# A macaron block with a recurrent mixer on one core: the mixer's TensorE order written out by hand, paired channel blocks, a split-row inverse, and chain steps moved to ScalarE

## The chip, the cores and the metric

The kernel runs on one core of one Trainium2 chip. The metric is device time in microseconds (us) of one execution. The engines are TensorE (PE: matmuls, and PEld: its weight loads), VectorE (DVE), ScalarE (ACT), GpSimd (POOL) and SyncE (SP), which issues the weight loads from DRAM.

## The reference

One transformer block on 256 tokens of width 2048, all in float32: a half-weighted SwiGLU, a mixer, and a second half-weighted SwiGLU, each between RMS norms.

```python
def _wkv7_scan(r, w, k, v, a, b):          # per head, state 64 x 64
    def step(state, inp):
        r_t, w_t, k_t, v_t, a_t, b_t = inp
        sa = jnp.einsum('bhvk,bhk->bhv', state, a_t)
        state = (state * w_t[:, :, None, :] + sa[..., None] * b_t[:, :, None, :]
                 + v_t[..., None] * k_t[:, :, None, :])
        return state, jnp.einsum('bhvk,bhk->bhv', state, r_t)
...
def _hybrid_mixer(u, w_in, ...):
    p = u @ w_in                            # 2048 -> 8480 columns
    z_a, z_b, g_a, g_b = jnp.split(p, IN_SPLITS, axis=-1)
    y_a = _rwkv7_branch(z_a, ...) @ w_proj_a
    y_b = _pool_branch(z_b, pool_w, pool_scale) @ w_proj_b
    m = jax.nn.sigmoid(g_a) * y_a + jax.nn.sigmoid(g_b) * y_b
    return m @ w_out
...
def reference(x, ...):
    f = _swiglu(_rmsnorm(h, ln_ffn1_pre[l]), ffn1_gate[l], ffn1_up[l], ffn1_down[l])
    h = h + 0.5 * _rmsnorm(f, ln_ffn1_post[l])
    mx = _hybrid_mixer(_rmsnorm(h, ln_mix_pre[l]), w_in[l], ...)
    h = h + _rmsnorm(mx, ln_mix_post[l])
    f = _swiglu(_rmsnorm(h, ln_ffn2_pre[l]), ffn2_gate[l], ffn2_up[l], ffn2_down[l])
    return h + 0.5 * _rmsnorm(f, ln_ffn2_post[l])
```

The recurrent branch has 16 heads of 64. It takes r, k, v, a decay, a gate and a learning rate from `z_a` after a token shift, runs the scan, normalizes, and adds a bonus. The pool branch subtracts each channel from its mean over the last 2, 4, 8 or 16 tokens (one window for each of four groups of 256 channels) and multiplies each group with a 256 x 256 matrix.

## The kernel before

**Products in three passes.** Every float32 weight tile (128 x 1024 numbers, 512 KB) is loaded by SyncE into one of four buffers (`w32`), cast on ScalarE to a high part `wH` (L101), and the rest `wL` is taken on VectorE (L102), into one of five buffers each. A product is then three matmuls, high by high, low by high, high by low (`mm3`, L109 to L111, 512 columns of output; L174 to L176 in the channel-major form, 256 columns). The casts and splits carry a high scheduling priority (`BOOST`).

**Stages.** Feed-forward 1 runs up to about 750 us of the span, the mixer from about 753 to 1420 us, feed-forward 2 after it. The change touches the mixer alone.

**The mixer.** `gemm_ch` makes channel-major blocks of 256 columns for the recurrent branch (the z blocks for k, v and r of each half of the heads) and for the pool windows; each block holds two PSUM banks, out of four for such products. `gemm_tok` makes the token-major gates and projections. `rwkv(hf, ...)` is the recurrent chain of one half, 8 heads. It replaces the 256-step scan by four chunks of 64 tokens:

- `pw`, `pa`: small products for decay and learning rate, sigmoids, a running sum, two exponentials;
- `pn`, GpSimd's power (L620), `pk`: the norm of k, turned back into channel-major form (L615 to L630);
- `pV`: transposes of v; `pA` (L706): products of the chunk's rows, masked into Xab, Xrb; `pB` (L720): transposes; `pb`: the bonus;
- the inverse of unit triangular matrices: four part transposes (L733), then 31 steps of a product (L740) and a sum (L742) on VectorE, two transposes back (L746, L747), and `pM`, `pX` to join 32 x 32 blocks into 64 x 64;
- the recurrence over four chunks: `pU` (L782), a copy (L789), `pSa` (L793), copies (L794, L795), `pS` (L800), the state update (L804, L805), `pY`, and the group norm;
- `pg`, `pT`: gate product and transposes back, and the branch's output `yT`.

The pool branch: `pool_window` computes a group's block, its product with the norm (L516), window sums (L522) and small fixes for the first tokens (L528 to L534), then the high and low parts `mxT` (L535, L536). `pool_mix` multiplies with the group's matrix (outputs `yb`, L547, L548). Group g's `pool_mix` is issued after group g+1's window; that of the last group is put off (`s.after`) until the next `gemm_ch` is done.

**What sets the order.** The source names the stages as `"a0 p a1 b0 b1 b2 b3"` (chain of half 0, pool, chain of half 1, then four blocks of the second projection), then four gate blocks. The order on every engine is made by the framework's scheduler, which plays the program through a model of the chip and takes instructions by readiness and priority. So TensorE's chain matmuls and the other products, called fillers here, are mixed by the scheduler. At run time each engine executes its instructions in that order.

Of the kernel before, what the change touches and what calls it, by code (L numbers as in the profile page):

```python
# [15 lines left out]
P = 128  # L16
# [18 lines left out]
ORDER = "a0 p a1 b0 b1 b2 b3"  # L35
# [9 lines left out]
class Block:  # L45
    def __init__(s, tc, ctx):
# [4 lines left out]
        s.after = []  # L51
# [98 lines left out]
    def gemm_pair(s, w, cols, at, KT, kh, evacs):  # L150

        pss = [[s.pm.tile([P, 512], F32, tag="mm", name=s.nm("mm")) for _ in range(2)]
               for _ in cols]
        for k0, k1 in ((0, kh), (kh, KT)):
            for i, c0 in enumerate(cols):
                for k, wH, wL in s.load_w(w, k0, k1 - k0, c0, 512):
                    xH, xL = at(k)
                    for h in range(2):
                        s.mm3(pss[i][h], xH[:, h * P:h * P + P], xL[:, h * P:h * P + P],
                              wH, wL, k == 0, k == KT - 1)  # L160
        for i in range(len(cols)):
            for h in range(2):
                evacs[i](h, pss[i][h])

    def gemm_ch(s, w, c0, cw, at, KT, evac, kstep):
        blocks = [(b, min(P, cw - b)) for b in range(0, cw, P)]
        pss = [s.pm.tile([P, 512], F32, tag="mm", name=s.nm("mc")) for _ in blocks]
        for k0 in range(0, KT, kstep):
            for k, wH, wL in s.load_w(w, k0, min(kstep, KT - k0), c0, cw):
                xH, xL = at(k)  # L170
                for (b, m), ps in zip(blocks, pss):
                    o = ps[:m, :S]
                    h_, l_ = wH[:, b:b + m], wL[:, b:b + m]
                    s.nc.tensor.matmul(o, h_, xH, start=k == 0, stop=False)  # L174
                    s.nc.tensor.matmul(o, l_, xH, start=False, stop=False)  # L175
                    s.nc.tensor.matmul(o, h_, xL, start=False, stop=k == KT - 1)  # L176
        with s.tc.high_priority(offset=BOOST):
            for i, (b, m) in enumerate(blocks):
                evac(i, pss[i][:m, :S])
        while s.after:  # L180
            s.after.pop()()
# [143 lines left out]
    def setup_mixer(s, prm):  # L325
# [40 lines left out]
        for h in range(2):  # L366
            for q, op in ((0, ALU.is_gt), (1, ALU.is_ge)):
                a = m[h * 64:h * 64 + 64, q]
                nc.gpsimd.affine_select(out=a, in_=a, compare_op=op, fill=0.0, base=0,
                                        pattern=[[1, C]], channel_multiplier=-1)  # L370
        s.bones = s.const([P, P], "bones")
# [3 lines left out]
        s.zi = 0  # L375
        s.zb = [s.const([P, S + 16], f"zb{i}") for i in range(2)]
        for z in s.zb:
            nc.gpsimd.memset(z[:, :16], 0.0)
# [4 lines left out]
    def shift(s, ps, m, mc, out):  # L383

        nc = s.nc
        z = s.tmp("z")[:m, :S]
        nc.vector.tensor_tensor(out=z, in0=ps, in1=s.rsb[:m], op=ALU.mult)
        zm = s.zb[s.zi % 2][:, 15:]
        s.zi += 1
        nc.scalar.activation(out=zm[:m, 1:], in_=z, func=AF.Copy,  # L390
                             scale=s.col["mu"][:m, mc:mc + 1])
        nc.vector.scalar_tensor_tensor(out=out, in0=z, scalar=s.col["omu"][:m, mc:mc + 1],
                                       in1=zm[:m, :S], op0=ALU.mult, op1=ALU.add)

    def mixer(s, prm, uT, rs, resid, emit, gpost, reload):
# [29 lines left out]
        def ev_l(i, ps):  # L425
            m = ps.shape[0]
            s.shift(ps, m, 24 + i, lz[:m, i])
            if i == 0:
                nc.scalar.activation(out=lz[:64, 0], in_=lz[:64, 0], func=AF.Tanh)
            else:  # L430
                nc.scalar.activation(out=lz[:m, i], in_=lz[:m, i], func=AF.Sigmoid)
        s.gemm_ch(w_in, 3 * W, 288, at, NKD, ev_l, 4)

        yT = [[s.unit((P, 4, S), F32R, n_) for n_ in ("yH", "yL")] for _ in range(2)]

        def branch_a(hf):
            z = {}
            for nme, zc in (("k", 1), ("v", 2), ("r", 0)):
                z[nme] = s.unit((P, 4, S), F32, "z" + nme)
                for b in range(2):  # L440
                    c0 = zc * W + hf * 512 + b * 256

                    def ev_z(i, ps):
                        s.shift(ps, P, c0 // P + i, z[nme][:, b * 2 + i])
                    s.gemm_ch(w_in, c0, 256, at, NKD, ev_z, 8)
            for t in yT[hf]:
                nc.scalar.copy(t[:, 0, :1], s.ident[:, :1])
            s.rwkv(hf, z["r"], z["k"], z["v"], lz, prm, *yT[hf])
# [7 lines left out]
        def branch_b(c):  # L456
            if c == 0:
                sg = [sgb0[:, 0], sgb0[:, 1]]
            else:
                sg = [s.tmp("sgb"), s.tmp("sgb")]  # L460
                s.gemm_tok(w_in, GB + c * 512, at, NKD, ev_sig(lambda h: sg[h]))
# [4 lines left out]
            while s.after:  # L466
                s.after.pop()()
            s.gemm_tok(prm["w_proj_b"], c * 512, at_b, NKW, ev_pb)

        for step in ORDER.split():  # L470
            if step == "p":
                mix = None
                for g, win in enumerate(POOL_WINDOWS):
                    nxt = s.pool_window(g, win, at, w_in)
                    if g:
                        pT.append(s.pool_mix(g - 1, mix, prm["pool_w"]))
                    mix = nxt
                s.after.append(lambda: pT.append(s.pool_mix(3, mix, prm["pool_w"])))
            elif step[0] == "a":
                branch_a(int(step[1]))  # L480
            else:
                branch_b(int(step[1]))

        sga = []
        for c in range(4):
            sg = s.unit((P, 2, 512), F32, "sga")
            sga.append(sg)
            s.gemm_tok(w_in, GA + c * 512, at, NKD, ev_sig(lambda h: sg[:, h]))
# [16 lines left out]
        s.gemm_pair(prm["w_proj_a"], (0, 512), at_a, NKW, 4, (ev_pa(0), ev_pa(1)))  # L505
# [4 lines left out]
    def pool_window(s, g, win, at, w_in):  # L510
        nc = s.nc
        mxT = s.unit((P, 2, 2, S), F32R, "mxT")

        def ev_b(i, ps):
            zp = s.zb[i]
            nc.vector.tensor_tensor(out=zp[:, 16:], in0=ps, in1=s.rsb, op=ALU.mult)  # L516
            cur = zp
            st = 1
            while st < win:
                nx = s.tmp("pl")[:, :S + 16]  # L520
                lo = 16 - (win - 2 * st)
                nc.vector.tensor_tensor(out=nx[:, lo:], in0=cur[:, lo:],  # L522
                                        in1=cur[:, lo - st:S + 16 - st], op=ALU.add)
                cur = nx
                st *= 2
            n = win - 1
            fx = s.small(16, "fx", bufs=2)[:, :n]
            nc.vector.tensor_tensor(out=fx, in0=cur[:, 16:16 + n], in1=s.rcp[:, :n],  # L528
                                    op=ALU.mult)
            nc.vector.tensor_tensor(out=fx, in0=fx, in1=zp[:, 16:16 + n], op=ALU.subtract)  # L530
            mx = cur[:, 16:]
            nc.vector.scalar_tensor_tensor(out=mx, in0=mx, scalar=1.0 / win,
                                           in1=zp[:, 16:], op0=ALU.mult, op1=ALU.subtract)
            nc.vector.tensor_copy(mx[:, :n], fx)  # L534
            nc.scalar.copy(mxT[:, 0, i], mx)  # L535
            nc.vector.tensor_tensor(out=mxT[:, 1, i], in0=mx, in1=mxT[:, 0, i].bitcast(F32),  # L536
                                    op=ALU.subtract)
        s.gemm_ch(w_in, RCOLS + g * 256, 256, at, NKD, ev_b, 8)
        return mxT

    def pool_mix(s, g, mxT, pool_w):
# [3 lines left out]
        def ev(i, ps):  # L545
            sc = s.col["pool_scale"][:, 2 * g + i:2 * g + i + 1]
            nc.scalar.activation(out=yb[:, 0, i], in_=ps, func=AF.Copy, scale=sc)  # L547
            nc.vector.scalar_tensor_tensor(out=yb[:, 1, i], in0=ps, scalar=sc,  # L548
                                           in1=yb[:, 0, i].bitcast(F32),
                                           op0=ALU.mult, op1=ALU.subtract)  # L550
        s.gemm_ch(pool_w[g], 0, 256, lambda k: (mxT[:, 0, k], mxT[:, 1, k]), 2, ev, 2)
        return yb[:, 0], yb[:, 1]

    def rwkv(s, hf, r, k, v, lz, prm, yH, yL):
# [25 lines left out]
        sw = reg(0, 4, S)  # L580
        for q in range(2):
# [22 lines left out]


        kk = reg(3, 4, S)
# [16 lines left out]
        nbf = nb.rearrange("p a b -> p (a b)")  # L623
        for q in range(2):
# [10 lines left out]
        for i in range(4):  # L635
            V.tensor_scalar(out=k2[:, i], in0=a[:, i], scalar1=col("k_a", i),
                            scalar2=col("oka", i), op0=ALU.mult, op1=ALU.add)
# [12 lines left out]
        E, O = slice(0, 64), slice(64, 128)  # L650
        t5 = (2, NCH, 2, C)
        BK = [reg(7, *t5), reg(8, *t5)]
        AR = [[reg(9, *t5), reg(10, *t5)], [reg(11, *t5), reg(12, *t5)]]
        EVs, ODs = reg(13, 4, NCH, C), reg(14, 4, NCH, C)
        Xab, Xrb = reg(4, 16, C), reg(5, 16, C)
        BKt = [reg(1, *t5), reg(2, *t5)]

        for q in range(2):
            pb = s.psum("pb").rearrange("p (i t) -> p i t", i=2)
            for i in range(2):  # L660
# [299 lines left out]
```

## Time and profile before

| | us |
|---|---|
| median of 3 runs | 2156.44 (2155.68 to 2157.66) |
| the profiled execution, its own time | 2156.19 |
| its span, first to last instruction | 2154.4 |

| engine | busy us | share of the span | instructions |
|---|---|---|---|
| TensorE matmul | 2114.6 | 98% | 11077 |
| weight loads | 1774.9 | 82% | 11077 |
| VectorE | 1288.9 | 60% | 1609 |
| ScalarE | 1086.2 | 50% | 1516 |
| GpSimd | 78.2 | 4% | 164 |

The mean granted TensorE clock of the execution is 0.992 of full speed. In the profile, L12 is line 12 of the kernel; a row of groups has line, engine, operation, output <- inputs, shape, count, then busy us and mean ns of one, then idle time of the engine before them and what ended it. Buffers are told by the program's names without their numbers: `R` is any of the chain's fifteen work tiles, `mc` a channel-major and `mm` a token-major PSUM tile.

### The profile page before, as it was taken

To read this page: it belongs to the slowest core of one execution; us is meant where nothing else is said; L and a number is where in the kernel's file an instruction comes from. 1 tells how busy PE (TensorE), PEld (TensorE's weight loads), DVE (VectorE), ACT (ScalarE), POOL (GpSimd) and SP (SyncE) were. 2 spreads that over 40 slices of the span, in tenths; PEclk is the share of its full clock that TensorE was granted. 3 is DMA by queue.
4 is the path that set the end of the run, shared out by engine and by line. 5 is a ranking of instruction groups with operands and counts; after the bars stand their busy time and mean duration, and the time that the engine had idled before them with its cause. 6 is when DMAs were issued, how large, how long until landed. Compare 5 with 4: busy or idle time off the path is not lost.

```text
span 2154.4 us, 28711 instructions
## 1 busy us (share of the span) xinstructions
PE 2114.6 (98%) x11077; PEld 1774.9 (82%) x11077; DVE 1288.9 (60%) x1609; ACT 1086.2 (50%) x1516; POOL 78.2 (4%) x164
## 2 busy tenths in 40 slices
PE   8999999999999999889999999999999999999998
PEld 6888888888888799889788778878888888888886
DVE  5556555555444556997689656565556555654444
ACT  6565556555444554444454434455565556554442
POOL 1000000000000100101110110010000000000000
PEclk9999999999999999999999999999999999999999
DMA  7656666667666666255556666656667666676664
GB/s 234 195 177 207 195 195 186 198 205 242 195 195 192 194 173 182 84 157 164 147 153 179 178 223 193 192 179 202 194 177 213 193 191 184 206 252 192 193 193 136
DMA packets 223219, 406.06 MB, mean 188 GB/s; under 512 B 12991, under 2 KB 48969, under 8 KB 223081
## 3 DMA queue, kind: packets, MB, share of 16 engines
q1 hardware_dynamic: 216937, 383.11, 58.9%
q0 software_dynamic: 6144, 21.11, 2.7%
q8 instruction: 87, 1.43, 0.3%
q14 instruction: 51, 0.42, 0.1%
HBM read 395.78 MB, written 8.39 MB: 188 GB/s over the span
## 4 chain that ended last, share of the span: by engine, by line
PE 90%; DVE 6%; issue 2%; ACT 1%; DMA 1%; POOL 0%; DVEq 0%; POOLq 0%; SPq 0%; ACTq 0%
PE mm L111 27%; PE mm L110 27%; PE mm L109 27%; PE mc L174 2%; PE mc L175 2%; PE mc L176 2%; DVE wL L102 2%; DVE R L733 1%; DVE pr L740 1%; DMA w<-in_ffn_gate_dram 1%; ACT wH L101 0%; DVE R L742 0%; PE tr L206 0%; DVE R L713 0%; ACT junk L239 0%
## 5 line engine op out<-in xcount | busy, mean ns | idle before, releaser
L102 DVE TENSOR_TENSOR wL<-w,wH 128x1024 fp32r<-128x1024 f32 (+2 forms) x734 | 884.9, 1212 | 768.7 <-ACT wH L101 767.5
L101 ACT CAST wH<-w 128x1024 fp32r<-128x1024 f32 (+2 forms) x734 | 761.0, 1043 | 901.0 <-PE mm L111 708.8
L109 PE MATMUL mm<-wH,xH 128*128 128x512 f32 x2496 | 974.9, 391 | 6.7 <-ACT xH L212 6.7
L111 PE MATMUL mm<-wH,xL 128*128 128x512 f32 x2496 | 975.4, 391 | 5.2 <-DVE xL L213 5.2
L110 PE MATMUL mm<-wL,xH 128*128 128x512 f32 x2496 | 974.4, 391 | 0.5 <-DVE wL L102 0.4
L109 PEld LDWEIGHTS mm<-wH,xH 128*128 128x128 f32 x2496 | 470.3, 188 | 107.3 <-ACT xH L212 9.7
L111 PEld LDWEIGHTS mm<-wH,xL 128*128 128x128 f32 x2496 | 470.2, 188 | 104.4 <-DVE xL L213 6.8
L110 PEld LDWEIGHTS mm<-wL,xH 128*128 128x128 f32 x2496 | 470.2, 188 | 98.8 <-DVE wL L102 1.4
L174 PE MATMUL mc<-xH,wH 128*128 128x256 f32 (+1 forms) x560 | 160.3, 287 | 5.0 <-DVE zb L516 5.0
L175 PE MATMUL mc<-xH,wL 128*128 128x256 f32 x560 | 160.4, 287 | 0.0
L176 PE MATMUL mc<-xL,wH 128*128 128x256 f32 x560 | 159.5, 285 | 0.0
L232 ACT COPY x<-T 32x256 f32<-32x256 f32 x352 | 141.9, 403 | 3.9
L174 PEld LDWEIGHTS mc<-xH,wH 128*128 128x128 f32 (+1 forms) x560 | 107.0, 191 | 6.2 <-issue 5.4
L175 PEld LDWEIGHTS mc<-xH,wL 128*128 128x128 f32 x560 | 107.1, 191 | 0.6
L176 PEld LDWEIGHTS mc<-xL,wH 128*128 128x128 f32 x560 | 107.1, 191 | 0.4
L251 ACT ACTIVATE sg<-mm,rs 128x512 f32<-128x512 f32 x44 | 30.2, 690 | 21.3 <-PE mm L111 21.3
L252 DVE SCALAR_TENSOR_TENSOR sg<-mm,rs,sg 128x512 f32<-128x512 f32 x44 | 31.6, 751 | 13.2 <-ACT sg L251 13.2
L283 POOL DMA_DIRECT2D gb<-in_ln_ffn_post_dram x4 | 2.2, 562 | 926.7 <-DVE xL L236 893.5
L239 ACT ACTIVATE junk<-mm 128x512 bf16<-128x512 f32 x24 | 14.3, 595 | 34.5 <-PE mm L111 34.5
L286 DVE TENSOR_TENSOR fg<-mm,gb 128x512 f32<-128x512 f32 x24 | 16.5, 691 | 24.5 <-ACT junk L239 24.5
L257 DVE SCALAR_TENSOR_TENSOR sg<-mm,rs,sg 128x512 f32<-128x512 f32 x44 | 30.9, 744 | 0.0
L222 DVE STREAM_TRANSPOSE T<-sg 128x512 f32<-128x512 f32 x44 | 30.9, 702 | 0.0
(220 smaller groups left out, 1030.2 us busy)
## 6 DMA issues: line engine op xcount, KB each, us to landing
w<-in_ffn_up_dram SPq DMA_DIRECT2D x176, 512.0 KB
w<-in_ffn_down_dram SPq DMA_DIRECT2D x176, 512.0 KB
w<-in_ffn_gate_dram SPq DMA_DIRECT2D x174, 512.0 KB
w<-in_w_in_dram SPq DMA_DIRECT2D x128, 512.0 KB
w<-in_w_out_dram SPq DMA_DIRECT2D x32, 512.0 KB
w<-in_w_proj_b_dram SPq DMA_DIRECT2D x16, 512.0 KB
w<-in_w_proj_a_dram SPq DMA_DIRECT2D x16, 512.0 KB
hsp<-fg POOLq DMA_DIRECT2D x16, 256.0 KB, 5.1
```

The lines of the kernel that those rows point to most:

```text
L101: nc.scalar.copy(vH, v)
L102: nc.vector.tensor_tensor(out=vL, in0=v, in1=vH.bitcast(F32), op=ALU.subtract)
L109: nc.tensor.matmul(ps, aH, bH, start=start, stop=False)
L110: nc.tensor.matmul(ps, aH, bL, start=False, stop=False)
L111: nc.tensor.matmul(ps, aL, bH, start=False, stop=stop)
L174: s.nc.tensor.matmul(o, h_, xH, start=k == 0, stop=False)
L175: s.nc.tensor.matmul(o, l_, xH, start=False, stop=False)
L176: s.nc.tensor.matmul(o, h_, xL, start=False, stop=k == KT - 1)
L222: s.nc.vector.transpose(out=T1[:, h * 512:h * 512 + 512], in_=src)
L232: nc.scalar.copy(dst[q * 32:q * 32 + 32, :, :, i], src[i * 32:i * 32 + 32, :, :, q])
L252: nc.vector.scalar_tensor_tensor(out=sg, in0=ps, scalar=rs[h], in1=sg, op0=ALU.mult, op1=ALU.mult)
L257: nc.vector.scalar_tensor_tensor(out=sig[h], in0=ps, scalar=rs[h], in1=sig[h], op0=ALU.mult, op1=ALU.mult)
```

## The change

1. TensorE's order in the mixer, from the first channel-major block to the end of the second chain, is the source's order. Products become generators that yield after every step with the time it is reckoned at (0.2265 us for a 512-column matmul, 0.12 for a 256-column one). The chain yields, ahead of each of its TensorE steps, how much filler is to stand before it. Fillers of chain 0: pool (p), b0, b1, the z blocks of half 1. Of chain 1: b2, b3, the four gate blocks, and the first half of the first pair of `w_proj_a` blocks. What is left of a list follows its chain. The other engines stay with the scheduler.
2. `pool_mix` of the last group now follows directly on that of the group before.
3. Channel-major blocks of 128 channels share a PSUM bank by twos, and are evacuated by one operation of twice the width where the scalar allows it. The buffer `zb` becomes one tile of two parts.
4. The inverse works on rows of which each covers two 16-wide halves, so that step kq handles `kq // 2 + 1` instead of `kq + 1` rows; the diagonal blocks are put down transposed by ScalarE (`Xd`), so that one full transpose takes the place of four; `Xo` holds the off-diagonal blocks.
5. From VectorE to ScalarE go: the swapped copy of v, the copies of `pV`, the scaled copies `kk` and `k2`, the copies of the inverse into `tt`. `pV` moves ahead of `pn`, `pb` behind `pB`, the load of `g2` ahead of the recurrence.

```diff
-ORDER = "a0 p a1 b0 b1 b2 b3"
+MM, MC = 0.2265, 0.12
...
+    def ch_g(s, w, c0, cw, at, KT, evac, kstep):
         blocks = [(b, min(P, cw - b)) for b in range(0, cw, P)]
-        pss = [s.pm.tile([P, 512], F32, tag="mm", name=s.nm("mc")) for _ in blocks]
+        banks = [s.pm.tile([P, 512], F32, tag="mm", name=s.nm("mc"))
+                 for _ in range(0, len(blocks), 2)]
...
+                    one = k == 0 and i % 2 == 0
+                    for n, (lh, rh) in enumerate(((h_, xH), (l_, xH), (h_, xL))):
+                        s.nc.tensor.matmul(o, lh, rh, start=one and n == 0,
+                                           stop=k == KT - 1 and n == 2,
+                                           skip_group_check=True)
+                    yield 3 * MC
...
+        def p_g():
+            mix = None
+            for g, win in enumerate(POOL_WINDOWS):
+                mxT = s.unit((P, 2, 2, S), F32R, "mxT")
+                yield from s.pool_window(g, win, at, w_in, mxT)
+                if g:
+                    yield from s.pool_mix(g - 1, mix, prm["pool_w"], pT)
+                mix = mxT
+            yield from s.pool_mix(3, mix, prm["pool_w"], pT)
...
+        def rest():
+            yield from p_g()
+            yield from b_g(0)
+            yield from b_g(1)
+            yield from z_g(1)
+
+        def rest1():
+            yield from b_g(2)
+            yield from b_g(3)
+            for c in range(4):
+                yield from ga_g(c)
+            for t in pair:
+                if t is None:
+                    return
+                yield t
+
+        def weave(steps, fill):
+            for need in steps:
+                while need > 0:
+                    t = next(fill, None)
+                    if t is None:
+                        break
+                    need -= t
+
+        with s.tc.manual_schedule(engines={mybir.EngineType.PE}):
+            for _ in s.ch_g(w_in, 3 * W, 288, at, NKD, ev_l, 4):
+                pass
+            for _ in z_g(0):
+                pass
+            for hf, fill in enumerate((rest(), rest1())):
+                weave(chain(hf), fill)
+                left = sum(fill)
...
     def rwkv(s, hf, r, k, v, lz, prm, yH, yL):
+        yield 4          # ahead of pw
+            yield 3      # ahead of each of two pV groups
+        yield 3          # ahead of pn
+        yield 9          # ahead of pk
+                yield ((20, 0), (3, 4))[q][i]      # ahead of each pA
+            yield (6, 4)[q]                        # ahead of each pB
+        yield 2          # ahead of pb
...
-            V.tensor_scalar(out=kk[:, i], in0=k[:, i], scalar1=col("k_k", i), scalar2=None,
-                            op0=ALU.mult)
+            A.activation(out=kk[:, i], in_=k[:, i], func=AF.Copy, scale=col("k_k", i))
...
-                    A.copy(Xab[R, g4], ps[R, :, 0])
+                    for o in (0, 32):
+                        A.copy(Xd[h * 64 + o:h * 64 + o + 32, :, g4]
+                               .rearrange("p t g -> p g t"),
+                               ps[h * 64 + o:h * 64 + o + 32, :, 0, o:o + 32])
+                    A.copy(Xo[h * 64:h * 64 + 32, g4], ps[h * 64:h * 64 + 32, :, 0, 32:])
...
-            V.transpose(out=wt[R], in_=Xab[R, :, o:o + 32].rearrange("p g t -> p t g")
-                        .unsqueeze(2).to_broadcast([32, 32, 2, 16]))
+        V.transpose(out=wt, in_=Xd.unsqueeze(2).to_broadcast([P, 32, 2, 16]))
...
-            n, m = kq + 1, 31 - kq
+            n, m = kq // 2 + 1, 31 - kq
...
+        yield 50         # ahead of pM
+        yield 3.5        # ahead of pX
+            yield 1.8 if c else 2.8                # ahead of each pU
+            yield 1.6                              # ahead of each pSa
+            yield 1.7                              # ahead of each pS, pY
+        yield 3          # ahead of pg
+        yield 5          # ahead of pT
```

(The words behind the yields are added here; they name the step that follows.)

More of the change, by code (lines that the diff above doesn't have):

```diff
@@ L370, in setup_mixer @@
                                         pattern=[[1, C]], channel_multiplier=-1)
+        s.dup = s.const([P, 2], "dup")
+        nc.vector.tensor_reduce(out=s.dup, in_=s.ident.rearrange("p (b d g) -> p d b g", b=4, d=2),
+                                axis=AX.XY, op=ALU.add)
         s.bones = s.const([P, P], "bones")
@@ L465, in ev_pb, with ga_g @@
                 nc.gpsimd.dma_start(out=msp[c, :, h], in_=sg[h])
[L466 to L482, printed above, removed]
+            yield from s.tok_g(prm["w_proj_b"], c * 512, at_b, NKW, ev_pb)
+        def p_g():
[7 more added lines that the diff above has]
+            yield from s.pool_mix(3, mix, prm["pool_w"], pT)
         sga = []
-        for c in range(4):
+        def ga_g(c):
             sg = s.unit((P, 2, 512), F32, "sga")
             sga.append(sg)
-            s.gemm_tok(w_in, GA + c * 512, at, NKD, ev_sig(lambda h: sg[:, h]))
+            yield from s.tok_g(w_in, GA + c * 512, at, NKD, ev_sig(lambda h: sg[:, h]))
         def at_a(k):
@@ L508, in mixer, with pool_window @@
         s.post(prm["w_out"], s.T_at(mT), NKD, gpost, 1.0, resid, emit, reload)
-    def pool_window(s, g, win, at, w_in):
+    def pool_window(s, g, win, at, w_in, mxT):
         nc = s.nc
[L512 to L528, printed above, removed]
-                                    op=ALU.mult)
[L530 to L539, printed above, removed]
@@ L541, in pool_mix, with ev_b @@
-    def pool_mix(s, g, mxT, pool_w):
+        def ev_b(banks):
+            nc.vector.tensor_tensor(out=s.zb[:, :, 16:], in0=banks[0],
+                                    in1=s.rsb.unsqueeze(1).to_broadcast([P, 2, S]),
+                                    op=ALU.mult)
+            for i in range(2):
+                zp = s.zb[:, i]
+                cur = zp
+                st = 1
+                while st < win:
+                    nx = s.tmp("pl")[:, :S + 16]
+                    lo = 16 - (win - 2 * st)
+                    nc.vector.tensor_tensor(out=nx[:, lo:], in0=cur[:, lo:],
+                                            in1=cur[:, lo - st:S + 16 - st], op=ALU.add)
+                    cur = nx
+                    st *= 2
+                n = win - 1
+                fx = s.small(16, "fx", bufs=2)[:, :n]
+                nc.vector.tensor_tensor(out=fx, in0=cur[:, 16:16 + n], in1=s.rcp[:, :n],
+                                        op=ALU.mult)
+                nc.vector.tensor_tensor(out=fx, in0=fx, in1=zp[:, 16:16 + n],
+                                        op=ALU.subtract)
+                mx = cur[:, 16:]
+                nc.vector.scalar_tensor_tensor(out=mx, in0=mx, scalar=1.0 / win,
+                                               in1=zp[:, 16:], op0=ALU.mult,
+                                               op1=ALU.subtract)
+                nc.vector.tensor_copy(mx[:, :n], fx)
+                nc.scalar.copy(mxT[:, 0, i], mx)
+                nc.vector.tensor_tensor(out=mxT[:, 1, i], in0=mx,
+                                        in1=mxT[:, 0, i].bitcast(F32), op=ALU.subtract)
@@ L542, in pool_mix @@
+        yield from s.ch_g(w_in, RCOLS + g * 256, 256, at, NKD, ev_b, 8)
+    def pool_mix(s, g, mxT, pool_w, pT):
         nc = s.nc
         yb = s.unit((P, 2, 2, S), F32R, "yb")
[L545 to L550, printed above, removed]
@@ L554, in rwkv @@
+        yield from s.ch_g(pool_w[g], 0, 256, lambda k: (mxT[:, 0, k], mxT[:, 1, k]), 2, ev,
+                          2)
+        pT.append((yb[:, 0], yb[:, 1]))
     def rwkv(s, hf, r, k, v, lz, prm, yH, yL):
@@ L696, in rwkv @@
                                 op=ALU.mult)
+        for t in (yH, yL):
+            A.copy(t[:, 0, :1], s.ident[:, :1])
         mb = s.mask.unsqueeze(1)
@@ L832, in rwkv @@
                             op=ALU.mult)
[L835 to L837 removed]
+        yield 3
+        pgs = []
         for q in range(2):
```

208 lines of the change are left out of this document (112 added, 96 removed).

## The prediction

> **What bounds the kernel now.** I read the busy time by stretches first, then TensorE's waits, then the granted clock around the long waits, then the groups of the mixer (753 to 1420 us). The columns of a stretch are its bounds, its length, then busy us and instruction count of TensorE, weight loads, VectorE, ScalarE and GpSimd, then the granted clock, the DMA share and GB/s.
>
> ```profile
> 800.00:850.00 50.00, 50.00 (x419) 50.00 (x418) 30.46 (x42) 22.18 (x30) 0.00 (x0) 1.00 0.67 184
> 850.00:900.00 50.00, 45.90 (x358) 44.28 (x357) 43.32 (x81) 23.13 (x36) 4.94 (x3) 0.96 0.42 113
> 900.00:950.00 50.00, 43.17 (x351) 41.79 (x351) 48.06 (x102) 18.03 (x28) 1.03 (x2) 0.94 0.40 116
> 950.00:1000.00 50.00, 48.85 (x454) 48.29 (x452) 48.32 (x89) 26.33 (x34) 2.75 (x4) 1.00 0.63 182
> 1350.00:1400.00 50.00, 50.00 (x222) 41.41 (x221) 26.42 (x28) 23.11 (x29) 0.00 (x0) 1.00 0.62 191
> ```
>
> TensorE is the bound: in undisturbed stretches it never stops. A 256-column matmul of a channel-major block is issued every 50/419 = 0.119 us, a 512-column one every 50/222 = 0.225 us. Between 850 and 1000 us, beside the first recurrent chain (up to its inverse), it stops, and there VectorE is full (48 of 50 us). All matmuls stay in the change, so what it can win or lose is TensorE's idle and slow time inside the mixer. The waits (total us, times, longest):
>
> ```profile
> PE mc L174 <- DVE zb L516: 5.0, 1, 5.0
> PE pA L706 <- DVE R L695: 3.8, 1, 3.8
> ...
> PE mc L174 <- DVE yb L548: 1.1, 1, 1.1
> PE pM L761 <- DVE R L746: 0.9, 1, 0.9
> PE pA L706 <- DVE R L713: 0.8, 1, 0.8
> PE pB L720 <- DVE R L713: 0.6, 1, 0.6
> PE pA L706 <- ACT R L724: 0.4, 1, 0.4
> ...
> PE pk L629 <- DVE R L622: 0.3, 1, 0.3
> ```
>
> These sum to 12.9 us: 12.0 in the first chain and 0.9 (pM) in the second. After three of them the granted clock is half:
>
> ```profile
> 896.07:902.90 6.83, 6.83 (x47) 6.38 (x47) 6.73 (x13) 1.10 (x3) 0.73 (x2) 0.50 0.67 205
> 926.79:930.20 3.41, 3.26 (x15) 3.29 (x16) 3.41 (x9) 0.00 (x0) 0.00 (x0) 0.50 0.61 165
> 1196.44:1199.86 3.42, 3.42 (x11) 2.74 (x9) 2.58 (x4) 3.37 (x4) 2.90 (x4) 0.50 0.44 105
> ```
>
> They follow the waits of 3.8, 5.0 and 0.9 us and last 6.8, 3.4 and 3.4 us. At half speed half of each is lost: 3.4, 1.7 and 1.7, in all 6.8 us. So the mixer loses 12.9 + 6.8 = 19.7 us. The profiled execution took 2156.19 us (span 2154.4), 0.25 below the median of the runs, 2156.44. With every wait gone it would take 2136.5 us; the forecast is that plus what the new order loses.
>
> **The change, part by part.** Durations used below (count, busy us, mean ns):
>
> ```profile
> L102 DVE TENSOR_TENSOR wL<-w,wH 128x1024 fp32r<-128x1024 f32 (+2 forms) x203 | 241.8, 1194 | 127.9 <-ACT wH L101 127.1
> L740 DVE TENSOR_TENSOR pr<-R,R 128x31 f32<-128x31 f32 (+15 forms) x62 | 29.7, 479 | 1.0
> L742 DVE TENSOR_TENSOR R<-R,pr 128x31 f32<-128x31 f32 (+15 forms) x62 | 21.3, 343 | 1.1
> L733 DVE STREAM_TRANSPOSE R<-R 32x1024 f32<-32x1024 f32 x8 | 16.2, 2027 | 0.1
> ...
> L687 DVE TENSOR_TENSOR R<-R,R 64x512 f32<-64x512 f32 x8 | 5.5, 686 | 0.1
> ...
> L522 DVE TENSOR_TENSOR pl<-pl 128x256 f32<-128x256 f32 (+3 forms) x12 | 5.2, 434 | 0.0
> ...
> L548 DVE SCALAR_TENSOR_TENSOR yb<-mc,cols,yb 128x256 fp32r<-128x256 f32 x8 | 3.7, 489 | 0.0
> ...
> L649 DVE TENSOR_TENSOR R<-R,R 128x1024 f32<-128x1024 f32 x2 | 2.4, 1205 | 0.0
> ...
> L528 DVE TENSOR_TENSOR fx<-pl,rcp 128x1 f32<-128x1 f32 (+3 forms) x8 | 1.3, 166 | 0.0
> L101 ACT CAST wH<-w 128x1024 fp32r<-128x1024 f32 (+2 forms) x203 | 208.4, 1027 | 273.1 <-PE mm L111 115.4 <-PE mc L176 96.9 <-DMA w<-in_w_in_dram 18.6
> L535 ACT CAST mxT<-pl 128x256 fp32r<-128x256 f32 x8 | 3.1, 404 | 9.1 <-DVE pl L534 9.0
> L620 POOL TENSOR_TENSOR n<-n,mhalf 128x16 f32<-128x16 f32 x2 | 7.7, 3837 | 124.6 <-DVE n L618 124.6
> L720 PE MATMUL pB<-ident,R 64*128 64x64 f32 x64 | 4.5, 244 | 0.6 <-DVE R L713 0.6
> ```
>
> *Inverse on split rows.* Per chain, 31 pairs of L740 and L742 take 31 × (0.479 + 0.343) = 25.5 us of VectorE. The rows a step works on are halved, the 62 instructions stay, so the new time lies between 12.7 and 25.5; I take 18. Four part transposes (L733, 8.1 us) become one of 2.0. The source puts 50.3 us of fillers ahead of pM. Beside them stand about 18 splits of 1.19 us, the transpose and the inverse: 21.5 + 2.0 + 18 = 41.5 us, under 50.3 even with 25.5 for the inverse (49.0). So pM's wait (0.9) and its half speed (1.7) go: 2.6 us in the second chain.
>
> *Paired blocks.* A 256-wide block takes one PSUM bank instead of two, so four can be open, not two. The 5.0 us wait for zb, where a new block waited for the bank of the one before, goes. Its two evacuations become one of twice the width, by L522 (256 columns) and L687 (512) 0.69 us instead of 2 × 0.43: nothing on the path.
>
> *Fixed order, fillers before pA.* 20.2 us of fillers now stand ahead of the first pA, so its waits on L695 and L713 go. But TensorE can no longer pass over a filler that is not ready, and the pool fillers feed each other through VectorE. Three places:
>
> (a) pk, the transposes that need the norm. The way is pn, L618, GpSimd's power (3.84 us), a copy, pk.
>
> ```profile
> 867.60 1.85 PE L615 MATMUL pn<-bones,R 128*128 128x2 f32 x16
> ...
> 879.46 1.09 PE L629 MATMUL pk<-ident,R 128*128 128x128 f32 x8 [0.30 <-DVE R L622]
> ...
> 1088.17 1.84 PE L615 MATMUL pn<-bones,R 128*128 128x2 f32 x16
> ...
> 1101.80 0.38 PE L629 MATMUL pk<-ident,R 128*128 128x128 f32 x2
> ```
>
> From the end of pn to pk it took 10.0 and 11.8 us (the rest over 3.84 is VectorE's queue ahead of L618). The source states 9.0 and 9.5 us. In the built order three weight splits still stand ahead of L618 in the second chain. So pk is late by 1.0 and 2.3 us. Bounds: 0, and 3 each.
>
> (b) The pool product of group 1 (mix 1). From the start of mix 0, TensorE reaches it after 12 + 96 matmuls, 12.9 us. Until its first input VectorE has, in the built order, 11 operations of 512 columns (7.5), one of 1024 (1.2), four window adds (1.7), one more as long as an add (0.4), eight small ones (1.3) and 5.5 splits (6.6): 18.7 us, then a ScalarE cast of 0.4. It is late by 6.2 us if none of these overlap. At least it is late by 3.6 us: the last split ahead needs a buffer that the last matmul before mix 1 frees, so cast 1.03, split 1.19, four small pool steps 0.9 and cast 0.4 follow it. I take 5.0. Its second half follows 1.3 us late (a 0.69 and a 0.49 us operation stand between). Sum 6.3.
>
> (c) The product of group 3 (mix 3) was held back until after the next z block; now it follows window 3 at once, with 12 matmuls of mix 2 (1.4) and the pB transposes (4.5/4 = 1.1) between: 2.5 us. VectorE needs the bank's product 0.7, seven window adds 3.0, two splits 2.4, three small ones 0.5, one more 0.4, and the cast 0.4: 7.4 us. Late by 4.9, or 2.5 if no split stands between; the second half 1.7 more. Sum 6.6.
>
> Waits of the first chain: 1.0 + 6.3 + 6.6 = 13.9 us, where there were 12.0. Half speed: the two long ones take the mean of what followed the waits of 3.8 and 5.0 us, 2.55 each; the short one 1.7, as after the wait of 0.9: 6.8, where there was 5.1. Second chain: pk 2.3 + 1.7 = 4.0, where there were 2.6.
>
> That a wait of 0.9 us is followed by 3.4 us at half clock is this trace's own. The Trainium skill, TensorE: Matmul & The Clock Gate section "Why this matters for your kernels", asks only that no idle gap exceed about 3 us. By that rule the two pk waits would cost no clock, and the sum would be 3.4 us lower, 2158.3. The trace disagrees at 1196 us, so the sum keeps them.
>
> *Chain steps on ScalarE.* The eight pV copies, the scaled copies and the split pA copies move from VectorE to ScalarE, which is busy 23 of 50 us in 850 to 900. I charge nothing beyond (a): the cover is that idle half. If it is gone, sigmoid, exponential and squares come later, up to the 3 us bound of (a).
>
> *Recurrent steps.* Between pU, pSa, pS and the next pU stand 1.8 to 2.2 us of fillers, 24 times.
>
> ```profile
> L804 DVE TENSOR_TENSOR st<-pS,R 64x256 f32<-64x256 f32 x12 | 5.0, 420 | 2.5 <-PE pS L800 2.3
> ...
> L794 DVE COPY R<-pSa 64x256 f32<-64x256 f32 x8 | 3.3, 414 | 6.2 <-PE pSa L793 6.2
> ...
> L789 ACT COPY us<-pU 128x256 f32<-128x256 f32 x8 | 3.0, 373 | 4.3 <-PE pU L782 4.3
> ```
>
> A copy of 0.37 behind one weight cast of 1.03 is 1.4 us: covered. The state update (four of 0.42) runs beside pY and the filler. pSa's copy (0.41, then ScalarE's of about 0.37) behind a split is 2.0 against 1.8: late by 0.2 at worst. I take 0.5 us for all; ends 0 and 15 (a second cast ahead of each, 1.4 + 1.03 − 1.8 = 0.6, times 24).
>
> Sum: 2136.5 + 13.9 + 6.8 + 4.0 + 0.5 = 2161.7; with the 0.25 to the median, 2162.
>
> **The rivals.** About 0.2% (4.3 us) is what a measurement of this kernel can tell from no change.
>
> *Even.* VectorE, relieved by some 14 us per chain (7.5 inverse, 6.1 transposes), clears its queue ahead of pn, and pk is in time in both chains: 1.0 + 1.7 + 4.0 less, 2155.3. For: in the first chain pk waited only 0.3 us. Against: the relief comes with the inverse, after pk.
>
> *Faster.* Besides, mix 1 is at its bound of 3.6 without half speed, and mix 3 at 2.5 + 1.7 with 1.7 of half speed: 9.5 + 0.5 us lost instead of 19.7, 2146.8. For: VectorE has no work of the inverse then, and its instructions may overlap more than I allow. Against: 48 of 50 us busy at 900 to 950.
>
> *Slower still.* A cast or split waiting for a buffer stands ahead of each recurrent copy, 0.6 us times 24: 2162 + 15 = 2177. It decides as soon as two casts pass the copy. For: both engines issue in order. Against: the weight queue runs several tiles ahead there.
>
> That the order isn't fixed as stated is excluded: the built program has TensorE's instructions in the source's order.
>
> **How the numbers follow.** Forecast 0.38 (own range 2161 to 2168, the upper ends of (a) and (b)), even 0.28 (2152.5 to 2160), faster 0.22 (2142 to 2152), slower still 0.12 (2168 to 2178). The range 2149 to 2171 leaves out most of the last and half of the faster case, some 0.2. Faster 0.22, same 0.28, slower 0.38 + 0.12 = 0.50.
>
> **What would show it.** In the changed profile: no wait of mc on zb and none of pA on the AR products; a wait of mc (mix 1) on the pool's VectorE steps of 4 to 6 us, one of mix 3 of 4 to 7 us, pk waiting 1 to 3 us in each chain, half clock after each; pM not waiting; recurrent groups without gaps. TensorE's waits in the mixer sum to about 17 us. If they sum to under 8, or the pool products do not wait, the forecast is wrong; if pU, pSa or pS lead the list, the third rival holds.

## The result and the profile after

The changed kernel takes 2147.5 us (median; 2146.5 to 2148.9) against 2156.4 (2154.7 to 2157.7): the ratio of the times is 0.9959, with a 95% interval of 0.9944 to 0.9973. The forecast was 2162, so the sign was wrong. The profiled execution took 2148.9 us (span 2147.2); it is the slowest of the five, 1.4 us over the median.

The stretches beside the first chain, after (columns as before):

```profile
850.00:900.00 50.00, 48.67 (x398) 47.60 (x397) 38.34 (x66) 29.44 (x48) 3.57 (x2) 1.00 0.43 129
900.00:950.00 50.00, 39.67 (x280) 35.23 (x280) 39.83 (x88) 25.21 (x52) 1.04 (x2) 0.83 0.38 118
950.00:1000.00 50.00, 50.00 (x281) 43.70 (x278) 43.60 (x90) 23.20 (x28) 4.83 (x8) 1.00 0.66 211
```

TensorE still stands still in the first two; VectorE is busy 38 to 40 of 50 us where it had 43 to 48. All waits of TensorE inside the mixer, after:

```profile
PE mc L194 <- ACT mxT L590: 10.3, 3, 5.3
PE pk L715 <- DVE pl L589: 1.1, 1, 1.1
PE pk L715 <- DVE R L707: 1.0, 1, 1.0
PE mc L194 <- DVE mxT L591: 0.2, 1, 0.2
```

They sum to 12.6 us; before it was 12.9. The waits on zb, on pA's inputs and of pM are gone; the pool products took their place. The long ones one by one, from the timeline (the wait in brackets):

```profile
907.26 0.58 PE L194 MATMUL mc<-mxT,wH 128*128 128x256 f32 x1 [5.28 <-ACT mxT L590]
932.27 0.58 PE L194 MATMUL mc<-mxT,wH 128*128 128x256 f32 x1 [4.66 <-ACT mxT L590]
934.36 0.58 PE L194 MATMUL mc<-mxT,wH 128*128 128x256 f32 x1 [0.39 <-ACT mxT L590]
```

These are mix 1, mix 3, and the second half of mix 3. The stretches at half clock, inside the mixer:

```profile
906.42:913.24 6.82, 5.98 (x27) 5.95 (x28) 6.66 (x25) 2.45 (x6) 0.00 (x0) 0.50 0.45 156
930.31:940.55 10.24, 7.89 (x34) 6.38 (x35) 6.20 (x20) 4.37 (x11) 0.00 (x0) 0.50 0.27 76
```

TensorE runs 5.98 + 7.89 us in them and loses half, 6.9 us; before it lost 6.8. So waits and half clock cost 19.5 us after and 19.7 before. By these two the change is worth nothing. Yet the same 4554 matmuls, from the first channel-major block of the chain to the end of the mixer, take less busy time. First before, then after:

```profile
770.20:1415.80 645.60, 632.29 (x4554) 552.03 (x4553) 472.58 (x750) 288.09 (x385) 46.48 (x65) 0.99 0.57 169
```

```profile
770.30:1407.80 637.50, 624.85 (x4554) 547.43 (x4553) 432.65 (x695) 310.75 (x453) 43.57 (x63) 0.99 0.54 172
```

The stretch is 8.1 us shorter, and 7.4 of them are TensorE's own work (632.3 to 624.9). The groups of the chain show whose. Before:

```profile
L706 PE MATMUL pA<-R,R 64*128 64x128 f32 x128 | 13.9, 309 | 5.0 <-DVE R L695 3.8 <-DVE R L713 0.8 <-ACT R L724 0.4
L782 PE MATMUL pU<-R,R 128*64 128x64 f32 x128 | 6.4, 230 | 0.0
```

```profile
L764 PE MATMUL pA<-R,R 64*128 64x128 f32 x128 | 9.7, 301 | 0.0
L783 PE MATMUL pB<-ident,R 64*128 64x64 f32 x64 | 2.9, 229 | 0.0
L857 PE MATMUL pU<-R,R 128*64 128x64 f32 x128 | 5.5, 228 | 0.0
```

After, pA takes 9.7 us for 13.9, pB 2.9 for 4.5, pU 5.5 for 6.4, with the same count and nearly the same duration of one. Some of these records ran at half clock in either trace. Counted from each start to TensorE's next start, without waits and with half clock counted as half, pA and pB together take 14.9 us before and 10.8 after. The timeline shows how; pA before and after, both at full clock:

```profile
1116.80 1.16 PE L706 MATMUL pA<-R,R 64*128 64x128 f32 x8
```

```profile
1145.02 1.16 PE L764 MATMUL pA<-R,R 64*128 64x128 f32 x16
```

Eight of them fill the time of sixteen. Each pA product uses 64 of the 128 rows. The source lets the two row halves take turns; then the two of a pair start 6 to 7 ns apart, and the next pair 105 ns later. In the order that the scheduler had built before, the first groups hold four products of one half in a run (two records each), and these start 112 ns apart; the last pA group (1127.04 us) already took turns. Over the records at full clock, pA's mean distance of starts falls from 88 to 65 ns, pB's from 56 to 40, pU's from 44 to 38.

### The profile page after: what moved, and what is told of

It reads as the page before. It is cut to its first block, busy times and chain, and to the rows that moved or that the text cites. A ratio compares the mean times of both kernels' runs of the same rounds, so it can differ in the third digit from the quotient of the medians.

```text
span 2147.2 us, 28719 instructions
## 1 busy us (share of the span) xinstructions
PE 2107.9 (98%) x11077; PEld 1771.6 (83%) x11077; DVE 1249.3 (58%) x1555; ACT 1109.3 (52%) x1584; POOL 75.4 (4%) x161
## 4 chain that ended last, share of the span: by engine, by line
PE 92%; issue 3%; DVE 2%; ACT 1%; DMA 1%; POOL 0%; DVEq 0%; POOLq 0%; SPq 0%; ACTq 0%
PE mm L109 27%; PE mm L110 27%; PE mm L111 27%; PE mc L194 7%; DVE wL L102 1%; DMA w<-in_ffn_gate_dram 1%; ACT wH L101 0%; PE pA L764 0%; PE tr L224 0%; ACT junk L257 0%; DVE fg L325 0%; PE pU L857 0%; PE pSa L869 0%; PE pY L892 0%; DVE pl L575 0%
## 5 line engine op out<-in xcount | busy, mean ns | idle before, releaser
L194 PE MATMUL mc<-xH,wH 128*128 128x256 f32 x560 | 161.2, 288 | 0.0
L194 PEld LDWEIGHTS mc<-xH,wH 128*128 128x128 f32 x560 | 106.6, 190 | 2.0 <-issue 0.7
```

What stands on the lines that cost most here:

```text
L194: s.nc.tensor.matmul(o, lh, rh, start=one and n == 0, stop=k == KT - 1 and n == 2, skip_group_check=True)
```

## The experiments

**The halves apart** (changed kernel):

```diff
-for c in range(NCH):
-    for h, R in ((0, E), (1, O)):
+for h, R in ((0, E), (1, O)):
+    for c in range(NCH):
         T.matmul(pAs[h][:, c], ...)          # and so for pB
```

> The changed kernel, with the loops of pA and pB turned so that the four products of one row half come before the four of the other; all else is kept. Theory A (side by side): in the trace of the changed kernel two pA products of different halves start 6 ns apart and the pair takes 112 ns, while in the trace before a run of one half takes 112 ns each. Eight pA groups of 8 pairs of records would cost 8 x 8 x 0.112 = 7.2 us more, less some 0.1 at each turn of the half, pB 1.2 us more; 1.8 us of it (the first two pA groups of chain 0) lies ahead of the wait for mix 3 and is swallowed by it. So 5.5 to 8 us slower than the changed kernel, 2153 to 2155.5, nearly all of the gain. Theory B (the gain is from waits and the inverse): within 1 us of the changed kernel, 2147.5.

2151.3 us, ratio to before 0.9975 (0.9965 to 0.9984): 3.8 us of the gain of 8.9 are gone. The interval of the ratio touches that of the changed kernel, so the rows carry the reading more than the times do. The waits on mxT and pk are the same to the tenth. Group and timeline:

```profile
L764 PE MATMUL pA<-R,R 64*128 64x128 f32 x128 | 13.9, 304 | 0.0
1149.94 1.71 PE L764 MATMUL pA<-R,R 64*128 64x128 f32 x16
```

Sixteen now take 1.71 us, not 1.16, and the group is back at 13.9 us. From start to start, as above, pA and pB take 14.7 us for 10.8: 3.9 more, as much as the time. I had expected 5.5 to 8 us: at each turn of the half one product of the new half still slips in beside the old, so the mean distance is 93 ns, not 107.

**The turns alone, in the kernel before**:

```diff
+with s.tc.manual_schedule(engines={mybir.EngineType.PE}):
     for c in range(NCH):
         for h, R in ((0, E), (1, O)):
             T.matmul(pAs[h][:, c], ...)      # and so for pB
```

> The kernel before, with only this done: within each pA group and each pB group TensorE takes the products in the source's order (the two halves in turn); where the groups stand among the fillers is still the scheduler's. Theory A (side by side): pA's mean pitch falls from 88 to 65 ns over 128 records and pB's from 56 to 40 over 64, so 3.0 + 1.0 = 4.0 us faster than before, about 2152.4, with the waits on zb, L695 and L713 still there (their sizes may move by 2 us). Theory B: no gain, 2156.4, as the floor would be the same.

2153.7 us, ratio 0.9987 (0.9979 to 0.9996): 2.7 us faster, of the 4.0 expected. The waits of pA grew (4.5 and 2.5 us for 3.8 and 0.8), and its row did not fall:

```profile
L707 PE MATMUL pA<-R,R 64*128 64x128 f32 x128 | 14.0, 339 | 7.0 <-DVE R L695 4.5 <-DVE R L714 2.5
```

Part of it ran at half clock, and the scheduler put fillers into the groups (two records at 1123.15 us, the other thirty from 1126.97). From start to start pA and pB take 13.2 us, where it was 14.9 before. So the trace shows 1.7 us for the turns here, against 3.9 in the changed kernel; where the rest of the 2.7 came from is not shown.

**Groups cut** (changed kernel; the fill stated beside each group is smaller by 0.6 to 0.7 us):

```diff
 for i in range(4):
+    if i == 2:
+        yield 0.6                 # pU, pSa; pY is cut between its two loops
```

> The changed kernel, with pU, pSa and pY of every chunk cut in two by 0.7 us of fillers, taken from the fill that stands ahead of the group or of the next one: 24 cuts, the same products in the same order otherwise. Theory A (every change between fillers and a chain group costs): in the trace of the changed kernel the last filler takes 318 ns to the next start where 227 is its pitch, the first pair of products 107 for 58, the last product 150 for 51, the first filler behind 338 for 227: 0.35 us in all, so 24 x 0.35 = 8 us slower, about 2155.5. Theory B (TensorE hides the change): within 1 us of 2147.5.

2154.2 us, ratio to before 0.9992 (0.9983 to 1.0001): 6.7 us more than the changed kernel for 24 cuts, 0.28 us each. In the timeline eight records of pU take 0.45 us where sixteen took 0.69. Before, the scheduler cut such groups (one product of pU, then fillers, then seven) and the fixed order does not. Between fillers, the chain's products stand in 58 stretches in the mixer before, in 54 after and in 78 here.

**The rest without the fixed order** (changed kernel):

```diff
-with s.tc.manual_schedule(engines={mybir.EngineType.PE}):
+if True:
```

> The changed kernel without the fixed order: TensorE's order is left to the scheduler again; paired blocks, split-row inverse, steps on ScalarE and the new order of emission stay. Theory A: the fixed order gives its gain by keeping the halves in turn and the chain groups whole. The order built here keeps the halves apart only in two pA groups and one pB group of chain 0, so it would lose 2 x 0.9 + 0.5 = 2.3 us by that, plus some 2 us of split recurrent groups, less what the scheduler saves by passing over the late pool products (waits 10.5 us in the changed kernel): 2140 to 2152. Theory B (the fixed fillers ahead of pA and pM are what counts): the waits of pA and pM come back, 2153 to 2158.

2156.8 us, ratio 1.0005 (0.9996 to 1.0014): paired blocks, split-row inverse and the steps on ScalarE are together worth nothing in time under the scheduler's order. The time is theory B's, but neither pA nor pM waits; the waits come back in other places:

```profile
PE pB L783 <- DVE R L775: 5.8, 2, 3.6
PE mc L194 <- ACT mxT L590: 2.4, 1, 2.4
PE pT L930 <- DVE R L908: 2.1, 1, 2.1
PE mm L109 <- ACT yH L938: 1.8, 1, 1.8
PE pSa L869 <- ACT us L864: 1.3, 1, 1.3
```

The mixer of the profiled execution (2159.7 us, the slowest of eleven) stands at half clock for 27.3 us, against 13.7 before. Yet pA's row is short:

```profile
L764 PE MATMUL pA<-R,R 64*128 64x128 f32 x128 | 9.0, 281 | 0.0
```

From start to start pA and pB take 12.3 us here, for 14.9 before. So a good part of the turns came with the new order of the source, without the fixed order, and longer waits and more half clock took back what they brought.

**The pool products later** (changed kernel; `b1` is the block's generator, `gap` draws from it):

```diff
+if g == 2:
+    yield from gap(10)                       # ahead of mix 1
 if g:
     yield from s.pool_mix(g - 1, ...)
...
+yield from gap(10)                           # ahead of mix 3
 yield from s.pool_mix(3, ...)
```

> The changed kernel, with 10 us of the gate block of b1 (needed by nobody here) moved ahead of the pool product of group 1 and 10 us more ahead of that of group 3; the fillers stated ahead of the chain's steps stay. Theory A: the two products wait only because their VectorE steps are 5.3 and 4.3 + 0.7 us late; with 10 us more ahead the waits go (10.3 us) and with them the half clock that follows (some 6.9 us lost): down to 17 us faster than the changed kernel, about 2131. Theory B (VectorE's queue is the bound): the added fillers bring four splits of 1.2 us each with them ahead of the pool's steps, which come as much later; 2 to 6 us of the waits stay and half clock too: 2138 to 2148.

2138.2 us, ratio 0.9918 (0.9905 to 0.9932): 9.3 us faster than the changed kernel, the fast end of theory B's range. Mix 1 no longer waits; mix 3 does, so does the block that reads it, and pk in both chains:

```profile
PE mm L109 <- DVE yb L615: 2.1, 1, 2.1
PE mc L194 <- DVE mxT L602: 1.7, 2, 1.5
PE pk L726 <- DVE R L718: 1.7, 1, 1.7
PE pk L726 <- DVE pl L600: 1.1, 1, 1.1
```

**The fillers spread by these waits**: `gap(6)` ahead of mix 1, 11 ahead of mix 3, 4.5 behind it, and `yield 12` for 9 ahead of pk.

> The changed kernel, with the gate block of b1 spread over three places: 6 us ahead of the pool product of group 1, 11 us ahead of that of group 3 (10 us left it 1.5 us late), 4.5 us behind it, ahead of the first block that reads its output (which waited 2.1 us with 10 and 10), and 12 us of fillers ahead of pk in both chains in place of 9 (waits 1.1 and 1.7 there). Theory A (what is late is late by what the trace shows): the waits of 6.7 us in the mixer go, and the 3.4 us at half clock: 2138.2 - 6.7 - 1.7 = 2130, 12 below the changed kernel's floor of waits or so. Theory B (each filler brings its own casts and splits, and the steps behind them come later again): 3 to 6 us of waits stay, 2134 to 2138.

2131.6 us, ratio to before 0.9881 (0.9866 to 0.9896): the lowest median, 15.9 us under the changed kernel. Only mix 0, which nothing had been put ahead of, still waits:

```profile
888.28 0.39 PE L194 MATMUL mc<-mxT,wH 128*128 128x256 f32 x1 [1.54 <-ACT mxT L602]
889.38 0.50 PE L194 MATMUL mc<-mxT,wH 128*128 128x256 f32 x2 [0.58 <-DVE mxT L603]
```

**Four places instead of three**: `gap(4)` ahead of mix 0 and of mix 1, 10 and 3.3 around mix 3, and again 12 ahead of pk.

> The changed kernel, with the gate block of b1 in four places: 4 us ahead of the pool products of groups 0 and 1, 10 us ahead of that of group 3, 3.3 us behind it, and 12 us of fillers ahead of pk. With 12 ahead of pk and nothing ahead of the product of group 0, that product waited 1.5 + 0.6 us and half clock for 3.4 us followed. Theory A: these 2.1 + 1.7 us go, and the mixer's TensorE has no wait left: about 2128. Theory B: with 4 in place of 6 us the product of group 1 waits again by about 2 us, and half clock returns: 2130 to 2133.

2132.5 us, ratio 0.9890 (0.9876 to 0.9903), the same within the intervals. Mix 0 is in time, mix 1 and mix 3 wait again (2.9 us on mxT), without half clock; and one pS and one pY wait 1.3 and 0.7 us for the copy of pSa on ScalarE. Theory A fell: the waits moved.

**Chain steps back on VectorE**, in the changed kernel, and in the version with four places:

```diff
-A.copy(ODs[E, :, c], po[E, :, 64:])
+V.tensor_copy(ODs[E, :, c], po[E, :, 64:])   # and the copy of v, kk, k2
```

> The changed kernel, with the swapped copy of v, the copies of pV into one half, and the scaled copies kk and k2 on VectorE again: per chain 4 x 0.41 + 2 x 0.42 + 4 x 0.34 + 4 x 0.41 = 5.5 us more of VectorE ahead of pA, and as much less of ScalarE. Theory A (VectorE's queue decides when the pool's steps come): mix 1 waits up to 5.5 us longer, pk too: 2149 to 2154. Theory B (VectorE had idle time there, 38 of 50 us busy at 850 to 900): the steps fall into it, 2146.5 to 2149.

2146.6 us, ratio 0.9956 (0.9944 to 0.9969): no loss; the move to ScalarE bought nothing here.

> The kernel of the run beside it (the gate block of b1 in four places, 12 us ahead of pk), with the swapped copy of v, half of the pV copies, kk and k2 on VectorE again. Theory A (those 5.5 us per chain fit into VectorE's idle time, as they did in the changed kernel, 2146.6 against 2147.5): within 1 us of the run beside it. Theory B (with the waits gone VectorE has less idle time there): pk and the pool products come late by up to 5 us: 2130 to 2136.

2136.4 us, ratio 0.9907 (0.9894 to 0.9921), 3.9 us more than the run beside it. But the mixer is as long in both traces (624.2 and 624.3 us). What differs lies outside it: half clock for 10.2 us at the mixer's start and 10.2 at its end, against 3.4 and 3.4. So this pair doesn't decide between the theories.

**The inverse made dearer** (changed kernel): the product of each step in a loop `for _ in range(2)`.

> The changed kernel, with each of the 31 products of the inverse (L810) made twice, the second time over the same numbers: 31 x 0.32 = 10 us more of VectorE per chain, more than the split rows saved (25.5 - 17.9 = 7.6). Theory A (the inverse is off the path): in the changed kernel the transpose behind the inverse of chain 1 ended at 1192.6 and pM started at 1210.8, 18 us later, so pM does not wait and the time stays within 1.5 us of 2147.5. Theory B (VectorE's work beside the second chain's fillers sets the pace): pM waits and the splits come late, 2150 to 2160.

2155.3 us, ratio 0.9992 (0.9983 to 1.0001): 7.8 us slower, so theory A fell. Chain 1 is unharmed, but in chain 0:

```profile
1004.61 2.01 PE L833 MATMUL pM<-R,R 32*32 32x32 f32 x64 [4.13 <-DVE R L821]
```

In the changed kernel the transpose that pM needs ended at 988.6 us, 16 us ahead of pM; here 16 us later, though only 10 us of work were added. Half clock for 6.8 us follows. What else delayed it I did not settle, and so it stays open whether the old inverse would make pM wait in the fixed order. The profiled execution was the fastest of the ten (2150.8 us), and its mixer is 4.4 us longer than that of the changed kernel; the rest of the 7.8 us is in no trace.

**Less filler ahead of pM** (changed kernel): `yield 31 if hf else 50`.

> The changed kernel, with 31 us of fillers ahead of pM in chain 1 in place of 50. pM is then reached at about 1191.8, and the transposed inverse is ready at 1192.6 to 1192.8: a wait of 0.5 to 1.5 us, as long as that of pM before (0.9) and as those of pk in the changed kernel (1.1 and 1.0, with no half clock behind them). Theory A (pM's 32 x 32 products count for the clock as if TensorE were idle, so that the wait and pM's 1.9 us together make some 3 us): half clock for 3.4 us behind pM, as in the trace before at 1196. Theory B (the wait's length alone decides, and about 1 us is too short): full clock behind pM, and the 3.4 us before had another cause.

One run, 2151.0 us. pM waits 0.85 us, and then (timeline, and the stretch behind it):

```profile
1192.51 1.98 PE L830 MATMUL pM<-R,R 32*32 32x32 f32 x64 [0.85 <-DVE R L818]
```

```profile
1194.91:1198.32 3.41, 3.41 (x10) 2.63 (x9) 0.70 (x1) 1.64 (x3) 0.00 (x0) 0.50 0.58 159
```

Half clock, as in the trace before at 1196 us, while the waits of 1.1 and 1.0 us ahead of pk cost no clock. So theory A: what counted was the wait together with pM's 2 us of 32 x 32 products. The last section shows that the place of the wait alone doesn't explain it.

## Why the prediction was wrong

**The step that failed is the floor**: "All matmuls stay in the change, so what it can win or lose is TensorE's idle and slow time". The matmuls stayed, but their order within a group sets what they take. With waits and half clock gone, the profiled execution would have taken 2148.9 - 12.6 - 6.9 = 2129.4 us, not 2136.5: 7.1 of the 12.8 us between the sum (2161.7) and the profiled 2148.9. The turns of the halves account for about 4 of them: pA and pB fell by 4.1 us from start to start, and putting the halves apart brought 3.9 back. Whole groups account for about 1.1 more: 0.28 us a cut, and four stretches fewer. The price is shown; that the four were cuts of the same kind is read from the orders. The last 2 us are only read from rows such as that of pU. The sign to see was in the built orders, put side by side: four pA products of one buffer in a row before, in turns after. I had looked in that order for fillers and waits, and not inside the groups. The signs of being wrong that I had named could not warn of it: the pool products did wait (5.3 and 4.7 us), and the waits summed to 12.6 us, over the 8 named. None of the signs was TensorE's busy time.

The Trainium skill, TensorEngine Tiling (Array Packing), section "Tiling Modes" states both: different tiles can work in parallel, and a change of the tiling mode drains TensorE. The trace agrees with the first, with 16 in 1.16 us against 8. The 0.28 us for a cut fit the second, but no run here shows that it is a drain. With these 7.1 us taken off, my sum would have been 2154.6, and without the half clock behind pk (below) 2151.2: faster than before.

**The other 5.7 us are sizes.** (a) pk: 1.0 forecast and 1.1 measured in chain 0, 2.3 and 1.0 in chain 1. Right in kind. The half clock behind both (1.7 each) did not come. I had read the 3.4 us behind pM's wait of 0.9 as a rule for every wait, and it was pM's own. By the rule on idle gaps of the Trainium skill, TensorE: Matmul & The Clock Gate, section "Why this matters for your kernels", which I had set aside, the sum would have been 3.4 us nearer. The last section has shorter gaps that did cost the clock.

(b) mix 1: 5.0 forecast, 5.28 measured; its second half 1.3 forecast, none measured. (c) mix 3: 4.9 forecast, 4.66 measured; second half 1.7, measured 0.39. The first halves came within 0.3 us. For mix 3 that is the queue counted by hand; for mix 1 the 5.0 was taken between bounds of 3.6 and 6.2, and that it fell so close is partly luck. The second halves were hardly late: VectorE's steps on the two halves stand in turn in the timeline. Half clock behind the two: 5.1 forecast, 6.9 measured.

*Inverse*: 18 us forecast; L810 and L812 sum to (20.1 + 15.7) / 2 = 17.9 per chain:

```profile
L810 DVE TENSOR_TENSOR pr<-R,R 128x126 f32<-128x126 f32 (+22 forms) x62 | 20.1, 323 | 1.5
L812 DVE TENSOR_TENSOR R<-R,pr 128x126 f32<-128x126 f32 (+22 forms) x62 | 15.7, 253 | 1.5
L803 DVE STREAM_TRANSPOSE R<-R 128x1024 f32<-128x1024 f32 x2 | 2.5, 1246 | 0.1
```

The one transpose took 1.2 us, not 2.0. pM did not wait, as forecast. Whether the cover would hold "even with 25.5" is open: with some 28 us for the inverse my sum gives 51.4 against 50.3 us, a wait of about 1 us in each chain, and pM waited 4.1 in chain 0 and not at all in chain 1.

*Paired blocks, pA's waits, recurrent steps*: the 5.0 us on zb and the waits of pA went; the recurrent groups ran without a wait (0.5 forecast). *The rivals*: slower still did not come. "Faster" named 2146.8, by a mix 1 and mix 3 with little half clock. The time came out there by another way: both waited as forecast.

## What to carry to other kernels

"No matmul is removed" does not fix TensorE's floor: where products use half of the rows, read in the built order whether the halves take turns and whether groups stay whole, and compare busy time over the same count. A wait that the trace names with its length can be bought off by moving a filler that nobody needs ahead of it, but the steps behind it move too; here two rounds of it took 15.9 us off. A wait that looks like a rule of the clock should be checked for what runs right behind it.

## What the runs showed of the hardware that was not expected

Half clock did not go by the length of one wait: 0.85 us and 2 us of 32 x 32 products brought it, so did 1.54 + 0.58 us within 2.7 us (the version with three places, 3.4 us at half clock from 890.0). Single waits of 1.0, 1.1 and 1.7 us did not, nor did 0.9 + 1.4 us within 3 us (the version with four places). All stretches at half clock that end inside the span last 3.4, 6.8, 10.2 or 13.7 us, and in each trace they start a whole number of steps of 10.24 / 3 = 3.4133 us apart, to 3 ns. The Trainium skill, TensorE: Matmul & The Clock Gate, section "What's actually happening", tells of a free-running window of 3413 ns; the lengths and the starts agree.

The traces also show what decides. Cut by that step from 760 to 1440 us, the thirteen traces give 2501 pieces at full clock. In 32 of them TensorE was idle for 2.05 us or more, and half clock followed every time. In 2461 it was idle for 1.56 us or less, and half clock followed twice: behind 0.87 and 0.85 us of idle with 1.9 and 2.0 us of pM in the same piece. Of the eight between 1.59 and 1.78 us, three were followed by it. So what counts is the idle time within one piece: the 1.54 + 0.58 us lie in one, the 0.9 + 1.4 us lie across an edge, 1.25 before and 1.05 behind it. pM alone costs nothing: 17 pieces with 1.7 us of it or more and no idle time were not followed by half clock.

Where the stretches fall changes with small shifts: at the mixer's two ends they lasted 3.4 and 3.4 us in one kernel and 10.2 and 10.2 in another with an equally long mixer, and the two times were 3.9 us apart. Differences of that size between two kernels can be such a shift, the 3.8 and 2.7 us above included; there the starts in the groups are the better evidence, and they give 3.9 and 1.7.
